# Keeping the split weights of the input and output projections in DRAM

## The chip, the cores and the metric

The kernel runs on one core of a Trainium2 chip. The metric is the time of one execution on the device, in microseconds (us). Three runs of the kernel before were timed; one more execution was recorded by the profiler, and all rows below are of that one.

## The reference

One layer of a hybrid decoder works on 2048 tokens of 1024 channels, in float32:

```
h    = rms_norm(x) * scale + shift
proj = h @ w_in                              # 1024 -> 3344 columns
o    = concat(gla(proj), rwkv7(proj))        # two recurrent mixers
x    = x + gate * (o @ w_out)                # 1024 -> 1024
x    = x + gate2 * conv_mlp(norm(x))         # gated MLP, width 2816
out  = rms_norm(x)
```

`scale`, `shift` and the gates come from one vector `c` through the modulation weights `ada_w`. The weights are the same for every token.

## The kernel before

**Split operands.** The projections want float32 accuracy from matmuls that take rounded operands (type `F32R`). So both sides are split into a high part, the rounded value, and a low part, the rest, and each product is three matmuls: high with high, low with high, high with low (`gemm3`, lines 258 to 265; the same three in `pair_gemm`, lines 431 to 433, and `values_tok`, lines 334 to 336).

**The class `Weights`** (lines 164 to 191) brings one tile of weights, 128 x 1024, in two halves of 128 x 512 (256 KB each). For each half a DMA on SyncE's queue (SP) fills a staging buffer `w_st` (line 174), ScalarE (ACT) casts it to the high part `w_hi` (line 179), and VectorE (DVE) or, every third time, GpSimd (POOL) subtracts to get the low part `w_lo` (line 182). In the first phase there are five staging buffers and three buffers each of `w_hi` and `w_lo` (line 158: `nst`, `nhl`). The modulation weights use the staging buffers too (`ada_dot`, line 200), without a split.

**Order of the work.** The tokens are four blocks of 512 (`NBLK`). First the modulation of block 0 is computed, with its Q, K and V projections straight from `w_first` (lines 533 to 560). Then `stage_b(b)` (lines 345 to 390) makes the other projections of a block: 18 tiles of `w_in` in block 0; 22 tiles of `w_in` and four tiles of `w_v` in blocks 1 to 3, so that every tile is loaded and split again in each block. The first two and the last two tiles of a block go in pairs (`pair_gemm`, lines 422 to 434), which ask for single halves (`cols=NB`). The results go to DRAM (`evacuate`).

The mixers work on 16 units of 128 tokens, `gla` (lines 610 to 726) and `rwkv_p`, `rwkv_i`, `rwkv_j`, `rwkv_s` (lines 751 to 1029). The projections of the next block are the filler between their steps: `fill()` (lines 395 to 408) advances `stage_b` by so many tiles per step. A unit's inverse goes out to DRAM and back twice, in other layouts (`inv_a`, lines 844 to 848; `inv_y`, lines 884 to 888), with DMAs on the same queue of SP. The modulation weights of the later stages are read five tiles per unit in the first units (`ada_rest`). When no block is left to project, the output projection `stage_d` (lines 436 to 471) of blocks 0 to 2 is the filler (`spare`, lines 1039 to 1046): eight tiles of `w_out` per block, split again for each.

The second phase, from line 1082 on, is the MLP, with other pools and buffers (line 1098: nine staging buffers and four each of `w_hi` and `w_lo`). The output projection of block 3 runs inside it (`d_begin`, line 1417), with `Weights` taking from these pools.

**What sets the order.** Each engine works through its instructions in a fixed order; the framework chooses it when the program is built, from priorities (`tc.cur_priority`, which `fill` sets back by `lag`) and its own estimate of when an instruction is ready. Waits between engines are semaphores. All DMAs here are issued by SP, in order, so one that waits holds up those behind it.

Of the kernel before, what the change touches and what calls it, by code (L numbers as in the profile page):

```python
# [9 lines left out]
F32 = mybir.dt.float32  # L10
F32R = mybir.dt.float32r
# [5 lines left out]
P = 128  # L17
D = 1024
KT = 8
NB = 512  # L20
# [9 lines left out]
TQ, TK, TV, TG, TZ, TR, TRK, TRV, TWA, TPG = 0, 2, 4, 8, 12, 13, 17, 21, 25, 26  # L30
# [65 lines left out]
def hybrid_kernel(ctx, tc, x, cst, vec, c_row, ada_t, w_in, w_v, w_first, w_z, gk_up, wa_up, g_up,  # L96
                  w_out, ffn_up, ffn_down, out, T=2048):
    nc = tc.nc
    NBLK = T // NB
# [55 lines left out]
        return ct[:, o - P:o - P + w]  # L155

    pools["w"] = ph1.enter_context(tc.tile_pool(name="wp1", bufs=2))
    pools["np"], pools["nst"], pools["nhl"], pools["nev"], pools["nx"] = 2, 5, 3, 3, 2
    pools["h"] = ph1.enter_context(tc.tile_pool(name="hp1", bufs=1))
    pools["hb"] = 9  # L160

    split_n = [0]

    class Weights:

        def __init__(self, src, split=True, cols=1024):
            n = pools["np"]
            step = 1024 // n
            self.step = step
            self.st, self.hi, self.lo = [], [], []  # L170
            for i in range((cols + step - 1) // step):
                w = min(step, cols - i * step)
                t = pools["w"].tile([P, step], F32, name="w_st", tag="wst", bufs=pools["nst"])
                nc.sync.dma_start(out=t[:, 0:w], in_=src[:, i * step:i * step + w])
                self.st.append(t)
                if split:
                    hi = pools["w"].tile([P, step], F32R, name="w_hi", tag="whi", bufs=pools["nhl"])
                    lo = pools["w"].tile([P, step], F32R, name="w_lo", tag="wlo", bufs=pools["nhl"])
                    A.copy(out=hi[:, 0:w], in_=t[:, 0:w])  # L179
                    split_n[0] += 1  # L180
                    eng = G if split_n[0] % 3 == 0 else V
                    eng.tensor_tensor(out=lo[:, 0:w], in0=t[:, 0:w], in1=hi[:, 0:w].bitcast(F32), op=ALU.subtract)  # L182
                    self.hi.append(hi)
                    self.lo.append(lo)

        def cut(self, which, a, n):
            i = a // self.step
# [68 lines left out]
    step = [0]  # L256
# [66 lines left out]
    def values_tok(b, h, i):  # L323

        bks = [gbank(), gbank()]
        for c in range(2):
            w = Weights(w_v[i, c])
            parts_ = [(k, t) for k in range(4) for t in range(4)] if c == 0 else [(k, t) for p_ in range(2) for k in range(4) for t in (2 * p_, 2 * p_ + 1)]
            for k, t in parts_:
                tc.cur_priority += step[0] // 4  # L330
                wh, wl = w.pair(k * 256, 256)
                hi, lo = (a_[:, t * P:(t + 1) * P] for a_ in h[4 * c + k])
                o_ = bks[t // 2][:, (t % 2) * 256:(t % 2) * 256 + 256]
                PE.matmul(out=o_, lhsT=hi, rhs=wh, start=c == 0 and k == 0 and t % 2 == 0, stop=False)
                PE.matmul(out=o_, lhsT=lo, rhs=wh, start=False, stop=False)
                PE.matmul(out=o_, lhsT=hi, rhs=wl, start=False, stop=c == 1 and k == 3 and t % 2 == 1)
            if c == 0:
                yield
        for p_ in range(2):
            ev = ap.tile([P, NB], F32, name="ev", tag="ev", bufs=pools["nev"])  # L340
            A.copy(out=ev, in_=bks[p_])
            nc.sync.dma_start(out=pd[b][TV][:, 2 * p_:2 * p_ + 2, i * 256:(i + 1) * 256], in_=ev.rearrange("p (t c) -> p t c", t=2))
        yield

    def stage_b(b):

        h = ahead.pop(b)[1]
        order = ([TZ] + list(range(8, TZ)) if b == 0 else list(range(8)) + [TZ] + list(range(8, TZ))) + [TWA, TPG] + [TR + i for i in range(12)]
        for i_, t in enumerate(order):
            if b + 1 < NBLK:  # L350
                if i_ == len(order) - 15:
                    ahead[b + 1] = stats_a(b + 1)
                if i_ == len(order) - 11:
                    stats_b(b + 1)
                if i_ == len(order) - 7:
                    stage_a(b + 1, range(0, EXTRA))
                if i_ == len(order) - 2:
                    stage_a(b + 1, range(EXTRA, KT))
            if t == TZ:

                ps = gbank()
                w = Weights(w_z, split=False, cols=KT * 32)
                for i in range(2):
                    for p_ in range(2):
                        for j in range(4):
                            k = 4 * i + j
                            PE.matmul(out=ps[32 * j:32 * j + 32], lhsT=w.cut(w.st, k * 32, 32), rhs=h[k][p_].bitcast(F32),
                                      start=i == 0 and p_ == 0, stop=i == 1 and p_ == 1)
                ev = ap.tile([P, NB], F32, name="ev", tag="ev", bufs=pools["nev"])
                A.activation(out=ev, in_=ps, func=AF.Identity, bias=vcol("zone"))  # L370
                nc.sync.dma_start(out=pd[b][TZ][:, 0, :], in_=ev)
                yield
                continue
            if TV <= t < TG:
                if (t - TV) % 2 == 0:
                    yield from values_tok(b, h, (t - TV) // 2)
                continue
            if b > 0 and i_ < 2:
                if i_ == 0:
                    bks = pair_gemm(w_in[0], w_in[1], h)  # L380
                ps = bks[i_]
            elif b + 1 < NBLK and i_ >= len(order) - 2:
                if i_ == len(order) - 2:
                    bks = pair_gemm(w_in[t - 1], w_in[t], h)
                ps = bks[i_ - len(order) + 2]
            else:
                ps = gbank()
                gemm3(ps, Weights(w_in[t if t < TZ else t - 1]), h)
            evacuate(b, t, ps)
            yield  # L390

# [27 lines left out]
            V.tensor_tensor(out=lo, in0=m, in1=hi.bitcast(F32), op=ALU.subtract)  # L419
        return h  # L420

    def pair_gemm(wa, wb, h):

        bks = [gbank(), gbank()]
        for c in range(2):
            ws = [Weights(w_[:, c * NB:(c + 1) * NB], cols=NB) for w_ in (wa, wb)]
            for k in range(4):
                hi, lo = h[4 * c + k]
                for ps, w in zip(bks, ws):
                    wh, wl = w.pair(k * P, P)  # L430
                    PE.matmul(out=ps, lhsT=wh, rhs=hi, start=c == 0 and k == 0, stop=False)
                    PE.matmul(out=ps, lhsT=wh, rhs=lo, start=False, stop=False)
                    PE.matmul(out=ps, lhsT=wl, rhs=hi, start=False, stop=c == 1 and k == 3)
        return bks

    def stage_d(b, h, acc=None, pair=False, before=None, after=None):
        if acc is None:
            acc = ap.tile([P, NB], F32, name="x_ss", tag="ns", bufs=1)
        bks = None
        for ft in range(KT):  # L440
            if pair and ft >= KT - 2:
                if bks is None:
                    if before is not None:
                        before()
                    bks = pair_gemm(w_out[ft], w_out[ft + 1], h)
                ps = bks[ft - KT + 2]
                if ft == KT - 1:
                    bks = None
            elif pair and ft < 2:
                if ft == 0:  # L450
                    bks = pair_gemm(w_out[0], w_out[1], h)
                ps = bks[ft]
                if ft == 1:
                    bks = None
            else:
                ps = gbank()
                gemm3(ps, Weights(w_out[ft]), h)
            if ft == 0 and after is not None:
                after()
            xr = ap.tile([P, NB], F32, name="xr", tag="xt", bufs=pools["nx"])  # L460
            nc.sync.dma_start(out=xr, in_=x[ft, :, b * NB:(b + 1) * NB])
            V.scalar_tensor_tensor(out=xr, in0=ps, scalar=mod[:, 16 + ft:17 + ft], in1=xr, op0=ALU.mult, op1=ALU.add)
            add_square(ap, acc, xr, ft == 0, G)
            nc.sync.dma_start(out=x2d[b][:, ft, :], in_=xr)
            if ft < KT - 1:
                yield
        fin = lambda: rstd_tok(rn2[:, b], sum_tok(acc))
        if pair:
            return fin
        yield  # L470
        fin()
# [31 lines left out]
    for i in range(4):  # L503
        hv, t_ = halves(i, "x0")
# [28 lines left out]
    for k in range(KT):  # L533
# [8 lines left out]
        hi, lo = hpair()  # L542
# [1009 lines left out]
```

## Time and profile before

| | us |
|---|---|
| median of 3 runs | 2959.83 |
| lowest and highest | 2950.89, 2960.01 |
| profiled execution | 2950.25 |
| its span, from the first to the last instruction | 2948.5 |

TensorE has two rows in the profile: PE is matmuls, PEld weight loads, which overlap them. A name with a small q (SPq) is an engine's queue of instructions. PEclk or "granted clock" is the share of full speed that TensorE had. In a group, "idle before" is the time that the engine stood idle just ahead of these instructions, followed by what ended it. The chain of waits goes back from the last instruction, at each step to what released it. L179 is line 179 of the kernel before. The execution runs in these stretches: opening and Q, K, V of block 0 until about 85 us; the other projections of block 0 until about 255; the mixers with the projections of blocks 1 to 3 until about 1090; the mixers with the output projection until about 1440; then the MLP, with the output projection of block 3 around 2090 to 2180.

### The profile page before, as it was taken

What the parts mean: (1) busy time and instruction counts of PE and PEld (TensorE: products, weight loads), DVE (VectorE), ACT (ScalarE), POOL (GpSimd) and SP (SyncE); (2) the same over time, 40 slices, a digit from 0 to 9 for tenths busy, and PEclk for the clock granted to TensorE, in tenths of its full rate; (3) what the DMA queues carried; (4) which work ended last, traced back from release to release, by engine and by line L of the source; (5) the groups of instructions that cost most, each with busy time, mean ns of one, the idle gap of its engine ahead of it and who ended that gap; (6) DMA issues with size and microseconds to landing.
All of it is one profiled execution on the core that took longest, in us unless ns stands there. A gap on an engine that the chain in (4) does not pass through costs nothing.

```text
span 2948.5 us, 54765 instructions
## 1 busy us (share of the span) xinstructions
PE 2764.5 (94%) x20296; PEld 2231.9 (76%) x20296; DVE 2198.3 (75%) x4229; ACT 1407.2 (48%) x2909; POOL 1189.5 (40%) x1212
## 2 busy tenths in 40 slices
PE   6998899999999999899869999999998999999998
PEld 5777777877777777777658788888776788888887
DVE  7368787777877677888587775866879786685867
ACT  4555445445554565555444353533545453353443
POOL 5224232323222233334455463544537454363541
PEclk9999999999989999989979999999998999999999
DMA  8556544544333334533415334243465534425243
GB/s 282 173 166 190 159 122 136 151 143 120 113 112 101 109 115 148 148 101 105 151 53 164 116 104 153 91 138 125 147 200 171 193 101 139 129 97 161 85 132 109
DMA packets 316875, 401.95 MB, mean 136 GB/s; under 512 B 75584, under 2 KB 148544, under 8 KB 316608
## 3 DMA queue, kind: packets, MB, share of 16 engines
q1 hardware_dynamic: 316608, 398.45, 43.2%
q8 instruction: 160, 2.62, 0.4%
q14 instruction: 107, 0.88, 0.1%
HBM read 293.49 MB, written 104.86 MB: 135 GB/s over the span
## 4 chain that ended last, share of the span: by engine, by line
PE 60%; DVE 15%; DMA 7%; issue 3%; ACT 2%; POOL 2%; SPq 0%; DVEq 0%; POOLq 0%; ACTq 0%
PE g_bank L1251 9%; PE g_bank L1249 9%; PE g_bank L1250 9%; PE g_bank L1306 5%; PE g_bank L1308 5%; PE g_bank L1307 5%; PE g_bank L263 3%; PE g_bank L265 3%; PE g_bank L264 3%; DMA w_st<-in_ada_t 1%; DVE w_lo L182 1%; PE gl_bank L679 1%; DMA x_k<-in_x 1%; DMA ub<-x 1%; DVE gl_d L652 1%
## 5 line engine op out<-in xcount | busy, mean ns | idle before, releaser
L1249 PE MATMUL g_bank<-h_hi,w_hi 128*128 128x512 f32 x1232 | 488.7, 397 | 29.0 <-ACT h_hi L1124 12.4
L1251 PE MATMUL g_bank<-h_hi,w_lo 128*128 128x512 f32 x1232 | 481.7, 396 | 16.8 <-POOL w_lo L1125 12.3
L1250 PE MATMUL g_bank<-h_lo,w_hi 128*128 128x512 f32 x1232 | 487.7, 396 | 7.7 <-DVE h_lo L1125 4.7
L1124 ACT CAST w_hi<-w_st 128x512 fp32r<-128x512 f32 (+1 forms) x396 | 239.1, 609 | 465.6 <-PE g_bank L1307 342.6
L1309 DVE SCALAR_TENSOR_TENSOR acc<-g_bank,mod,acc 128x512 f32<-128x512 f32 (+1 forms) x200 | 144.9, 729 | 249.5 <-PE g_bank L1308 234.5
L1125 POOL TENSOR_TENSOR w_lo<-w_st,w_hi 128x512 fp32r<-128x512 f32 x154 | 221.5, 1439 | 229.2 <-ACT w_hi L1124 225.5
L263 PE MATMUL g_bank<-h_hi,w_hi 128*128 128x512 f32 x736 | 299.3, 408 | 5.2 <-ACT carry L320 3.8
L265 PE MATMUL g_bank<-h_hi,w_lo 128*128 128x512 f32 x736 | 297.4, 405 | 3.5 <-DVE w_lo L182 3.5
L1249 PEld LDWEIGHTS g_bank<-h_hi,w_hi 128*128 128x128 f32 x1232 | 235.5, 191 | 84.3 <-ACT h_hi L1124 14.7
L264 PE MATMUL g_bank<-h_lo,w_hi 128*128 128x512 f32 x736 | 295.9, 402 | 0.0
L1251 PEld LDWEIGHTS g_bank<-h_hi,w_lo 128*128 128x128 f32 x1232 | 235.7, 191 | 71.6 <-POOL w_lo L1125 17.8
L1250 PEld LDWEIGHTS g_bank<-h_lo,w_hi 128*128 128x128 f32 x1232 | 235.8, 191 | 58.9 <-DVE h_lo L1125 5.7
L1306 PE MATMUL g_bank<-hh,w_hi 128*128 128x512 f32 x640 | 251.5, 395 | 4.7 <-DVE acc L1309 4.6
L1308 PE MATMUL g_bank<-hh,w_lo 128*128 128x512 f32 x640 | 251.5, 395 | 0.0
L1307 PE MATMUL g_bank<-hl,w_hi 128*128 128x512 f32 x640 | 251.4, 395 | 0.0
L179 ACT CAST w_hi<-w_st 128x512 fp32r<-128x512 f32 x272 | 167.6, 619 | 118.8 <-PE g_bank L264 59.9
L182 POOL TENSOR_TENSOR w_lo<-w_st,w_hi 128x512 fp32r<-128x512 f32 x90 | 128.3, 1425 | 228.6 <-ACT w_hi L179 191.5
L1125 DVE TENSOR_TENSOR w_lo<-w_st,w_hi 128x512 fp32r<-128x512 f32 (+1 forms) x242 | 201.1, 831 | 19.4 <-ACT w_hi L1124 19.4
L182 DVE TENSOR_TENSOR w_lo<-w_st,w_hi 128x512 fp32r<-128x512 f32 x182 | 142.2, 782 | 63.6 <-ACT w_hi L179 52.9
L263 PEld LDWEIGHTS g_bank<-h_hi,w_hi 128*128 128x128 f32 x736 | 141.1, 192 | 37.5 <-ACT carry L320 4.8
L265 PEld LDWEIGHTS g_bank<-h_hi,w_lo 128*128 128x128 f32 x736 | 141.1, 192 | 36.1 <-DVE w_lo L182 5.2
L264 PEld LDWEIGHTS g_bank<-h_lo,w_hi 128*128 128x128 f32 x736 | 141.6, 192 | 28.7 <-issue 0.5
(344 smaller groups left out, 6382.1 us busy)
## 6 DMA issues: line engine op xcount, KB each, us to landing
acc<-acc SPq DMA_DIRECT2D x352, 256.0 KB, 3.1
w_st<-in_ffn_up SPq DMA_DIRECT2D x176, 256.0 KB, 3.0
w_st<-in_w_in SPq DMA_DIRECT2D x168, 256.0 KB, 3.0
proj<-ev SPq DMA_DIRECT2D x100, 256.0 KB, 3.0
w_st<-in_ffn_down SPq DMA_DIRECT2D x80, 256.0 KB, 2.7
w_st<-in_ada_t SPq DMA_DIRECT2D x64, 256.0 KB, 3.4
w_st<-in_w_out SPq DMA_DIRECT2D x64, 256.0 KB, 3.1
x_k<-in_x SPq DMA_DIRECT2D x48, 256.0 KB, 3.7
```

Source lines behind the costliest of these rows:

```text
L182: eng.tensor_tensor(out=lo[:, 0:w], in0=t[:, 0:w], in1=hi[:, 0:w].bitcast(F32), op=ALU.subtract)
L263: PE.matmul(out=ps, lhsT=wh, rhs=hi, start=k == 0, stop=False)
L264: PE.matmul(out=ps, lhsT=wh, rhs=lo, start=False, stop=False)
L265: PE.matmul(out=ps, lhsT=wl, rhs=hi, start=False, stop=k == KT - 1)
L1124: A.copy(out=hi, in_=t)
L1125: eng.tensor_tensor(out=lo, in0=t, in1=hi.bitcast(F32), op=ALU.subtract)
L1249: PE.matmul(out=ps, lhsT=wh[:, c], rhs=hi, start=first and k == 0, stop=False, skip_group_check=True)
L1250: PE.matmul(out=ps, lhsT=wh[:, c], rhs=lo, start=False, stop=False, skip_group_check=True)
L1251: PE.matmul(out=ps, lhsT=wl[:, c], rhs=hi, start=False, stop=last and k == 3, skip_group_check=True)
L1306: PE.matmul(out=ps, lhsT=wh, rhs=hh, start=j == 0, stop=False)
L1307: PE.matmul(out=ps, lhsT=wh, rhs=hl, start=False, stop=False)
L1308: PE.matmul(out=ps, lhsT=wl, rhs=hh, start=False, stop=j == n - 1)
```

## The change

`Weights` gets a key for each tile. At the first use of a keyed half, the half is loaded and split as before, and its high and low parts are also stored in DRAM, in two tiles of 256 KB, by two more DMAs on SP. At a later use of the same key both parts are loaded straight into `w_hi` and `w_lo` by two DMAs, with no staging buffer, cast or subtraction. The last block stores nothing that no later block uses. The first projection of block 0 (`w_first`), the small weights `w_z` and the modulation weights have no key. The first phase has four staging buffers instead of five, and six buffers each of `w_hi` and `w_lo` instead of three.

```diff
--- before.py
+++ after.py
@@ -155,21 +155,32 @@
         return ct[:, o - P:o - P + w]
 
     pools["w"] = ph1.enter_context(tc.tile_pool(name="wp1", bufs=2))
-    pools["np"], pools["nst"], pools["nhl"], pools["nev"], pools["nx"] = 2, 5, 3, 3, 2
+    pools["np"], pools["nst"], pools["nhl"], pools["nev"], pools["nx"] = 2, 4, 6, 3, 2
     pools["h"] = ph1.enter_context(tc.tile_pool(name="hp1", bufs=1))
     pools["hb"] = 9
 
     split_n = [0]
 
+    kept = {}
+
     class Weights:
 
-        def __init__(self, src, split=True, cols=1024):
+        def __init__(self, src, split=True, cols=1024, key=None, at=0, keep=True):
             n = pools["np"]
             step = 1024 // n
             self.step = step
             self.st, self.hi, self.lo = [], [], []
             for i in range((cols + step - 1) // step):
                 w = min(step, cols - i * step)
+                if split and (key, at + i) in kept:
+                    pair = []
+                    for s_, from_ in zip(("hi", "lo"), kept[key, at + i]):
+                        t = pools["w"].tile([P, step], F32R, name="w_" + s_, tag="w" + s_, bufs=pools["nhl"])
+                        nc.sync.dma_start(out=t.bitcast(F32), in_=from_)
+                        pair.append(t)
+                    self.hi.append(pair[0])
+                    self.lo.append(pair[1])
+                    continue
                 t = pools["w"].tile([P, step], F32, name="w_st", tag="wst", bufs=pools["nst"])
                 nc.sync.dma_start(out=t[:, 0:w], in_=src[:, i * step:i * step + w])
                 self.st.append(t)
@@ -182,6 +193,13 @@
                     eng.tensor_tensor(out=lo[:, 0:w], in0=t[:, 0:w], in1=hi[:, 0:w].bitcast(F32), op=ALU.subtract)
                     self.hi.append(hi)
                     self.lo.append(lo)
+                    if key is not None and keep:
+                        to = []
+                        for s_, t in (("hi", hi), ("lo", lo)):
+                            d_ = dram.tile([P, step], F32, name=f"k{s_}_{len(kept)}")
+                            nc.sync.dma_start(out=d_, in_=t.bitcast(F32))
+                            to.append(d_)
+                        kept[key, at + i] = to
 
         def cut(self, which, a, n):
             i = a // self.step
@@ -324,7 +342,7 @@
 
         bks = [gbank(), gbank()]
         for c in range(2):
-            w = Weights(w_v[i, c])
+            w = Weights(w_v[i, c], key=("v", i, c), keep=b + 1 < NBLK)
             parts_ = [(k, t) for k in range(4) for t in range(4)] if c == 0 else [(k, t) for p_ in range(2) for k in range(4) for t in (2 * p_, 2 * p_ + 1)]
             for k, t in parts_:
                 tc.cur_priority += step[0] // 4
@@ -377,15 +395,16 @@
                 continue
             if b > 0 and i_ < 2:
                 if i_ == 0:
-                    bks = pair_gemm(w_in[0], w_in[1], h)
+                    bks = pair_gemm(w_in, 0, "in", h, b + 1 < NBLK)
                 ps = bks[i_]
             elif b + 1 < NBLK and i_ >= len(order) - 2:
                 if i_ == len(order) - 2:
-                    bks = pair_gemm(w_in[t - 1], w_in[t], h)
+                    bks = pair_gemm(w_in, t - 1, "in", h, b + 1 < NBLK)
                 ps = bks[i_ - len(order) + 2]
             else:
                 ps = gbank()
-                gemm3(ps, Weights(w_in[t if t < TZ else t - 1]), h)
+                t_ = t if t < TZ else t - 1
+                gemm3(ps, Weights(w_in[t_], key=("in", t_), keep=b + 1 < NBLK), h)
             evacuate(b, t, ps)
             yield
 
@@ -419,11 +438,11 @@
             V.tensor_tensor(out=lo, in0=m, in1=hi.bitcast(F32), op=ALU.subtract)
         return h
 
-    def pair_gemm(wa, wb, h):
+    def pair_gemm(wsrc, t0, name, h, keep):
 
         bks = [gbank(), gbank()]
         for c in range(2):
-            ws = [Weights(w_[:, c * NB:(c + 1) * NB], cols=NB) for w_ in (wa, wb)]
+            ws = [Weights(wsrc[t][:, c * NB:(c + 1) * NB], cols=NB, key=(name, t), at=c, keep=keep) for t in (t0, t0 + 1)]
             for k in range(4):
                 hi, lo = h[4 * c + k]
                 for ps, w in zip(bks, ws):
@@ -442,19 +461,19 @@
                 if bks is None:
                     if before is not None:
                         before()
-                    bks = pair_gemm(w_out[ft], w_out[ft + 1], h)
+                    bks = pair_gemm(w_out, ft, "out", h, True)
                 ps = bks[ft - KT + 2]
                 if ft == KT - 1:
                     bks = None
             elif pair and ft < 2:
                 if ft == 0:
-                    bks = pair_gemm(w_out[0], w_out[1], h)
+                    bks = pair_gemm(w_out, 0, "out", h, True)
                 ps = bks[ft]
                 if ft == 1:
                     bks = None
             else:
                 ps = gbank()
-                gemm3(ps, Weights(w_out[ft]), h)
+                gemm3(ps, Weights(w_out[ft], key=("out", ft)), h)
             if ft == 0 and after is not None:
                 after()
             xr = ap.tile([P, NB], F32, name="xr", tag="xt", bufs=pools["nx"])
```

## Rows read from the trace of the kernel before

**Rows 1.** The page: span, busy time of each engine, chain by engine.

```profile
span 2948.5 us, 54765 instructions
...
PE 2764.5 (94%) x20296; PEld 2231.9 (76%) x20296; DVE 2198.3 (75%) x4229; ACT 1407.2 (48%) x2909; POOL 1189.5 (40%) x1212
...
PE 60%; DVE 15%; DMA 7%; issue 3%; ACT 2%; POOL 2%; SPq 0%; DVEq 0%; POOLq 0%; ACTq 0%
```

**Rows 2.** Busy time by stage: PE, PEld, DVE, ACT, POOL, PEclk, DMA share, GB/s.

```profile
0.00:85.00 85.00, 59.41 (x252) 45.02 (x253) 59.53 (x88) 41.21 (x67) 38.53 (x37) 0.98 0.80 279
85.00:255.00 170.00, 159.12 (x1058) 128.42 (x1056) 102.95 (x248) 89.55 (x205) 49.98 (x67) 0.99 0.52 165
255.00:650.00 395.00, 366.26 (x4126) 296.26 (x4127) 306.48 (x832) 198.77 (x485) 119.83 (x142) 0.94 0.50 149
650.00:1090.00 440.00, 421.49 (x4714) 336.40 (x4713) 332.25 (x926) 236.23 (x588) 131.44 (x177) 0.95 0.37 110
1090.00:1440.00 350.00, 328.68 (x3816) 264.17 (x3816) 262.60 (x715) 184.55 (x462) 125.97 (x138) 0.93 0.43 130
1440.00:1540.00 100.00, 63.36 (x319) 47.65 (x318) 77.74 (x96) 46.36 (x80) 58.25 (x47) 0.76 0.28 87
```

**Rows 3.** The chain of waits from 255 to 1440 us, summed by line.

```profile
by line: PE g_bank L263 6.3%; PE g_bank L264 6.2%; PE g_bank L265 6.2%; issue 5.1%; DMA w_st<-in_ada_t 2.7%; DVE w_lo L182 2.2%; PE gl_bank L679 1.9%; DMA x_k<-in_x 1.9%; DVE gl_d L652 1.6%; PE rp_bank L113 1.4%; DMA inv_a<-rw_mab 1.4%; DVE
```

**Rows 4.** The page's costliest groups: the split of the weights.

```profile
L179 ACT CAST w_hi<-w_st 128x512 fp32r<-128x512 f32 x272 | 167.6, 619 | 118.8 <-PE g_bank L264 59.9
L182 POOL TENSOR_TENSOR w_lo<-w_st,w_hi 128x512 fp32r<-128x512 f32 x90 | 128.3, 1425 | 228.6 <-ACT w_hi L179 191.5
...
L182 DVE TENSOR_TENSOR w_lo<-w_st,w_hi 128x512 fp32r<-128x512 f32 x182 | 142.2, 782 | 63.6 <-ACT w_hi L179 52.9
```

**Rows 5.** Line 179 alone by stage: ACT busy (casts), PEclk, DMA share, GB/s.

```profile
85.00:255.00 170.00, 26.69 (x43) 0.99 0.52 165
255.00:650.00 395.00, 41.41 (x67) 0.94 0.50 149
650.00:1090.00 440.00, 46.50 (x75) 0.95 0.37 110
1090.00:1440.00 350.00, 31.90 (x52) 0.93 0.43 130
2090.00:2180.00 90.00, 9.61 (x16) 1.00 0.54 173
```

**Rows 6.** Line 263 (matmul): duration in ns, min/median/max.

```profile
L263 PE MATMUL g_bank<-h_hi,w_hi x736: 387/389/796, 82.4 to 2178.3; 128*128 128x512 f32 x184
```

**Rows 7.** Groups by line, 2090 to 2200 us: busy, mean ns, idle before, releaser.

```profile
L265 PE MATMUL g_bank<-h_hi,w_lo 128*128 128x512 f32 x64 | 25.3, 396 | 3.1 <-DVE w_lo L182 3.1
L263 PE MATMUL g_bank<-h_hi,w_hi 128*128 128x512 f32 x64 | 25.0, 391 | 1.1 <-ACT w_hi L179 1.1
```

**Rows 8.** DMA issues of the whole run: count, KB each, median us to landing.

```profile
w_st<-in_w_in SPq DMA_DIRECT2D x168, 256.0 KB, 3.0
...
w_st<-in_w_first SPq DMA_DIRECT2D x16, 256.0 KB, 6.1
...
rw_ln<-inv_a SPq DMA_DIRECT2D x32, 32.0 KB, 2.1
```

**Rows 9.** Line 174 on SP's queue: issue in ns, min/median/max, first and last start.

```profile
L174 SPq DMA_DIRECT2D w_st<-in_ada_t x64: 327/328/1298, 199.9 to 680.8; - x64
```

**Rows 10.** Waits of SP's queue, 255 to 1090 us: total us, times, longest.

```profile
SPq L174 <- DVE w_lo L182: 84.7, 44, 7.4
SPq L174 <- POOL w_lo L182: 45.6, 18, 6.4
```

**Rows 11.** Waits of ACT, 255 to 1090 us: total us, times, longest.

```profile
ACT w_hi L179 <- PE g_bank L264: 27.4, 21, 2.8
...
ACT w_hi L179 <- PE g_bank L335: 15.2, 13, 2.4
```

**Rows 12.** The chain in order of time: start us, us, what.

```profile
1441.86 5.63 DMA w_st<-in_ffn_up
```

## The prediction

> **What bounds the kernel now.** The page's first lines come first: of a span of 2948.5 us PE is busy 2764.5 us (94%), and the chain that ended last is 60% PE, 15% DVE, 7% DMA [rows 1]. A saving on ACT, DVE or POOL therefore counts only where PE is made to wait. The table of busy time by stage says where that is [rows 2]. I cut the span at 85, 255, 1440 and 1540 us: the opening, the projections of block 0 (from 85), the mixers with the projections of blocks 1 to 3 and the output projections beside them (255 to 1440), the change to the MLP. Before 255 us PE is short of full by 10.9 us only (159.12 of 170). From 255 to 1440 us it is busy 366.26 + 421.49 + 328.68 = 1116.4 of 1185 us: 68.6 us idle, with the granted clock at 0.94, 0.95 and 0.93 and DVE busy 306.48 + 332.25 + 262.60 = 901.3 us, 76%. This stage can gain from the change. The chain there is mixed: the three lines of the big matmuls have 19%, and of the work that the change removes the subtraction on DVE has 2.2%, 26 us of 1185 [rows 3]. So PE, DVE and waits take turns; no single engine bounds the stage.
>
> **What the change removes.** Splitting a half tile costs an ACT cast of 619 ns (272 of them) and a subtraction, 782 ns on DVE (182) or 1425 ns on POOL (90) [rows 4]. By the code, split work stays for the 16 halves of the first projection, 36 of block 0, 16 of block 1 (Q, K, V) and 16 of the output projection: 84. The other 188 become loads. The casts by stage are 43 from 85 to 255 us, 67 + 75 + 52 = 194 from 255 to 1440 us and 16 in the MLP's part [rows 5], so 272 - 210 = 62 lie before 255 us; 84 - 62 = 22 stay after it, and 172 of the 194 go. That is 172 x 0.619 = 106 us of ACT, 115 x 0.782 = 90 us of DVE and 57 x 1.425 = 81 us of POOL, all beside PE. What of it reaches the end? From below, nothing: PE would find the next late thing, the mixers' own DVE operations. From above, all idle time and what the low clock costs. DVE's busy share falls from 76% to 811/1185 = 68%; if waiting grows as share/(1 - share), which is my choice of a curve, it falls from 3.18 to 2.17, by 32%. 32% of 68.6 us is **22 us**; 89% of the chain's 26 us, 23 us, says the same by another way. I take 22.
>
> **The clock.** A 128x512 matmul takes 389 ns at the median and 796 ns at most [rows 6], which are the levels of 2.4 and 1.2 GHz. A mean grant of 0.94 over 1185 us is about 141 us at the lower level, so at most 70 us lost, PE's idle time included. Fewer gaps should raise the grant. 32% of 70 is 22 us; I take half, **11 us**, since a gap that only shrinks can still be followed by slow matmuls. Ends: 0 and 32 us.
>
> **The output projection inside the MLP.** Its last block has 16 halves. PE waited 3.1 us for the subtraction and 1.1 us for the cast there [rows 7]: **4 us** less. Each half now needs two loads into four buffers shared with the MLP's own weights, instead of one load into nine; a landing of 256 KB takes 3.0 us [rows 8], so two late ones would eat the gain (end: +6).
>
> **What it adds.** Each of the 188 halves loads twice, and 68 halves are stored in two parts: 188 + 136 = 324 transfers of 256 KB, 85 MB over the 402 moved now. In block 0 all is bunched: the 43 casts between 85 and 255 us bring 86 stores, 22.5 MB in 170 us, and 165 GB/s become about 298. The opening moves 279 GB/s at a DMA share of 0.80 [rows 2], and a weight load lands there in 6.1 us against 3.0 us elsewhere [rows 8]. Hidden by what? Loads run ahead by four staging and six split buffers, ten halves of twelve matmuls (4.7 us each), against three split buffers before. If that cover fails and the DMA stays at 279 GB/s, the 170 us become 182: +12. From below: the six buffers end the present waits of the cast for PE; but PE is full there, so 0. I take **+4**. Later the added transfers number 172 + 44 stores, 57 MB in 1185 us, 48 GB/s on about 129: no bound.
>
> SP's queue is the other cost. An issue takes 328 ns [rows 9], so 216 x 0.328 = 71 us more in the stage, on a queue where SP already stands still for 84.7 us behind DVE's subtraction and 45.6 us behind POOL's, before the loads of L174, from 255 to 1090 us alone [rows 10]. These waits go. In their place a kept load waits until PE has finished with the buffer six halves back, and what is queued behind it on SP waits too: the units' loads and the two trips through DRAM for the inverse. The nearest row for such a hold is ACT's wait for PE ahead of the cast: 27.4 + 15.2 us in 34 times, 1.25 us each, with three buffers [rows 11]. With six it should be rarer. Below zero is possible (holds vanish, ACT is freed); above see the rival. I take **+5**.
>
> The change to the MLP at 1440 us has PE busy 63.36 of 100 us [rows 2], and its chain starts with a 5.63 us weight load [rows 12]. The first pool of weights grows by 10 KB per partition, so the later pools wait for other tiles than before; I take 0, ends -6 and +6.
>
> **Sum.** -22 - 11 - 4 + 4 + 5 = -28 us. The profiled execution took 2950.25 us (span 2948.5), so 2922. The median of the three runs is 9.6 us above it (two near 2960, one at 2951); I add half: **2927 us**.
>
> **Rivals.** (1) **More comes free** than the 32%. Beside the splits the chain has 2.7% (32 us) on the staged loads of the modulation weights [rows 3]. They share the five staging buffers with the input projection, whose loads stand in the same queue. Kept halves leave that ring, so these 32 us can go as well, and the clock's 32 instead of 11: -22 - 32 - 32 - 4 + 4 + 5 = -81, 2869 + 5 = 2874. For it speaks that the waits named for L174 are those of this ring; against it that the last of the modulation's loads is issued at 680.8 us [rows 9] and that PE idles only 28.7 us up to 650. Chance 0.18.
>
> (2) **Hidden anyway.** PE is 94% busy, and the order of each engine is fixed when the program is built; PE could wait for the mixers' DVE operations as long as now. Then only the 4 us and the costs are left: 2950 + 5, 2955 to 2960. For it: 2.2% is all that the chain shows of the subtraction on DVE, and PE's own lines have 19%. Chance 0.14.
>
> (3) **Slower: SP's queue turns into the wait.** The place is L174 between 255 and 1440 us, the price h per hold. A unit passes SP at five places on its serial way (the load of its inputs, then out and back twice); the rows have 32 loads of rw_ln, two a unit, so 16 units and 80 places [rows 8]. If each meets one held load and half of that is covered by units prepared ahead, it costs 40h. It decides from 40h = 33 us (the gain without SP's 5 us), h = 0.83 us. At 1.5 us, somewhat over ACT's present 1.25: 2950 - 33 + 60 = 2977, and 2982 with the 5. For it: two parts per half wait for PE, in order, on a queue that already waits much. Against it: twice the buffers, and 130 us of other waits removed from the same queue. Chance 0.19.
> The Trainium skill (DMA: Bandwidth & Descriptors, Latency and other measured facts) gives an HBM access as 0.2 us on average and 2 us at high load: by it, an estimate, the 80 places at half cover cost up to 40 x 1.8 = 72 us, 2989 us. The opening's 6.1 against 3.0 us agrees in direction [rows 8]; no row shows the trips of the inverse under such load, so this adds to rival 3 and not to the sum.
>
> That the change does nothing is excluded: every later use has the key and the half of the first use, in pairs as well as in single tiles.
>
> **Numbers.** The forecast itself has 0.49, about 2905 to 2945. A difference of 0.3% (9 us) is about what the runs can tell from none; they span 9.1 us. Faster by more: 0.18 + 0.47 + a little of rival 2 = 0.66; within 0.3%: 0.15; slower: 0.19. The range goes from rival 1 (2875) up to nearly rival 3 at h = 1.5: 2875 to 2975.
>
> **What would show it.** Right: 84 casts on L179 and as many subtractions; DVE busy about 90 us less from 255 us on; PE idle in that stage near 47 us and the granted clock above 0.95; SP's waits behind the subtractions nearly gone; block 0 as long as now. Wrong: PE's idle time in the stage unchanged with other releasers (rival 2); SP's waits for PE's matmuls before the kept loads, and DVE waiting longer for rw_ln and rw_y (rival 3); block 0's projections ending 10 us later with landings near 6 us (the store's cover).

## The result

The changed kernel took 2935.04 us at the median of six runs, the kernel before 2949.32 us beside it. The ratio is 0.9941, with a 95% interval of 0.9921 to 0.996: 0.6% less time, some 17 us. The forecast was 2927 us, 0.8% below the 2950 us of the profiled execution; its sum had 28 us less.

**The profile after.** First the page of the changed kernel: span, busy time by engine, the chain by engine. They answer to [rows 1].

```profile
span 2925.2 us, 54728 instructions
...
PE 2751.4 (94%) x20296; PEld 2229.9 (76%) x20296; DVE 2085.8 (71%) x4103; ACT 1298.4 (44%) x2721; POOL 1088.3 (37%) x1150
...
PE 69%; DVE 13%; DMA 9%; ACT 3%; issue 3%; POOL 2%; SPq 0%; DVEq 0%; POOLq 0%; ACTq 0%
```

DVE, ACT and POOL each work 100 to 113 us less. PE's share of the span is what it was. The chain's shares, 69% for PE instead of 60%, cannot be set side by side as they stand: in the kernel before the chain can be followed back to 302 us only, where its first piece (start, length) is

```profile
301.96 4.54 DMA rw_k<-proj
```

while in the changed kernel it goes back to the start, through the opening and block 0. From 320 us to the first matmul of the MLP, with the pieces added up, PE has 47% of the chain before and 55% after, and DVE 28% and 18%.

Fixed cuts in time no longer fit, since every stage moves. I cut both traces at events instead: the first matmul of block 0's projections (L263, in the changed kernel L281), the first of the value projection of block 1 (L334, now L352) and the first of the MLP (L1249, now L1268). The first of these for the kernel before is in [rows 6]. The column after the durations is the first and last start, us. Before:

```profile
L334 PE MATMUL g_bank<-w_hi,h_hi x192: 274/283/467, 252.0 to 910.5; 128*128 128x256 f32 x192
L1249 PE MATMUL g_bank<-h_hi,w_hi x1232: 387/389/797, 1454.6 to 2889.7; 128*128 128x512 f32 x176
```

After:

```profile
L281 PE MATMUL g_bank<-h_hi,w_hi x736: 386/390/796, 80.6 to 2152.5; 128*128 128x512 f32 x184
L352 PE MATMUL g_bank<-w_hi,h_hi x192: 274/283/582, 240.6 to 891.2; 128*128 128x256 f32 x192
L1268 PE MATMUL g_bank<-h_hi,w_hi x1232: 387/389/797, 1423.3 to 2867.0; 128*128 128x512 f32 x176
```

Busy time between these cuts, kernel before (columns as in [rows 2]):

```profile
82.40:252.00 169.60, 161.25 (x1071) 130.30 (x1067) 99.95 (x245) 89.24 (x205) 47.49 (x66) 0.99 0.52 167
252.00:1454.60 1202.60, 1125.72 (x12795) 904.68 (x12794) 910.84 (x2485) 627.91 (x1551) 389.23 (x465) 0.94 0.44 131
1454.60:2948.50 1493.90, 1420.74 (x6196) 1154.06 (x6196) 1127.97 (x1413) 649.52 (x1090) 714.22 (x646) 0.97 0.41 130
```

and changed kernel:

```profile
80.60:240.60 160.00, 148.77 (x908) 121.72 (x905) 82.84 (x199) 77.13 (x179) 40.79 (x56) 0.96 0.93 321
240.60:1423.30 1182.70, 1126.91 (x12963) 911.99 (x12961) 824.09 (x2414) 539.94 (x1401) 307.08 (x417) 0.95 0.59 181
1423.30:2925.20 1501.90, 1419.42 (x6194) 1153.54 (x6192) 1117.97 (x1403) 640.36 (x1075) 701.22 (x642) 0.97 0.41 132
```

All that was won was won before the MLP: 31.3 us, of which the MLP's part gives 8.0 us back. The first stretch is 9.6 us shorter, but it holds 163 PE instructions fewer and the second 168 more: the mixers' work moved across the cut. So the first two belong together: 1372.2 us became 1342.7. PE's idle time in them fell from 85.2 to 67.0 us, and its busy time, for as many matmuls, from 1287.0 to 1275.7 us.

### The profile page after: what moved, and what is told of

It reads as the page before. It is cut to its first block, busy times and chain, and to the rows that moved or that the text cites. A ratio compares the mean times of both kernels' runs of the same rounds, so it can differ in the third digit from the quotient of the medians.

```text
span 2925.2 us, 54728 instructions
## 1 busy us (share of the span) xinstructions
PE 2751.4 (94%) x20296; PEld 2229.9 (76%) x20296; DVE 2085.8 (71%) x4103; ACT 1298.4 (44%) x2721; POOL 1088.3 (37%) x1150
## 4 chain that ended last, share of the span: by engine, by line
PE 69%; DVE 13%; DMA 9%; ACT 3%; issue 3%; POOL 2%; SPq 0%; DVEq 0%; POOLq 0%; ACTq 0%
PE g_bank L1270 9%; PE g_bank L1268 9%; PE g_bank L1269 9%; PE g_bank L1325 5%; PE g_bank L1327 5%; PE g_bank L1326 5%; PE g_bank L281 4%; PE g_bank L283 4%; PE g_bank L282 4%; PE gl_bank L698 1%; DMA rw_k<-proj 1%; DMA acc<-acc 1%; PE g_bank L450 1%; DMA w_st<-in_ada_t 1%; PE g_bank L452 1%
## 5 line engine op out<-in xcount | busy, mean ns | idle before, releaser
L1268 PE MATMUL g_bank<-h_hi,w_hi 128*128 128x512 f32 x1232 | 488.0, 396 | 26.6 <-ACT h_hi L1143 14.8
L1144 POOL TENSOR_TENSOR w_lo<-w_st,w_hi 128x512 fp32r<-128x512 f32 x154 | 219.3, 1425 | 241.7 <-ACT w_hi L1143 237.9
L281 PE MATMUL g_bank<-h_hi,w_hi 128*128 128x512 f32 x736 | 299.0, 406 | 8.0 <-DMA w_hi<-khi 3.8
L1268 PEld LDWEIGHTS g_bank<-h_hi,w_hi 128*128 128x128 f32 x1232 | 235.1, 191 | 81.6 <-ACT h_hi L1143 18.0
L1325 PE MATMUL g_bank<-hh,w_hi 128*128 128x512 f32 x640 | 251.9, 396 | 6.0 <-DVE acc L1328 6.0
L281 PEld LDWEIGHTS g_bank<-h_hi,w_hi 128*128 128x128 f32 x736 | 140.3, 191 | 41.6 <-issue 4.5
L1325 PEld LDWEIGHTS g_bank<-hh,w_hi 128*128 128x128 f32 x640 | 120.1, 188 | 37.3 <-DVE acc L1328 6.9
L1327 PEld LDWEIGHTS g_bank<-hh,w_lo 128*128 128x128 f32 x640 | 120.2, 188 | 29.4
L1326 PEld LDWEIGHTS g_bank<-hl,w_hi 128*128 128x128 f32 x640 | 120.2, 188 | 29.1
```

The costliest lines, as they stand in the source:

```text
L281: PE.matmul(out=ps, lhsT=wh, rhs=hi, start=k == 0, stop=False)
L1144: eng.tensor_tensor(out=lo, in0=t, in1=hi.bitcast(F32), op=ALU.subtract)
L1268: PE.matmul(out=ps, lhsT=wh[:, c], rhs=hi, start=first and k == 0, stop=False, skip_group_check=True)
L1325: PE.matmul(out=ps, lhsT=wh, rhs=hh, start=j == 0, stop=False)
L1326: PE.matmul(out=ps, lhsT=wh, rhs=hl, start=False, stop=False)
L1327: PE.matmul(out=ps, lhsT=wl, rhs=hh, start=False, stop=j == n - 1)
```

## The experiments

Four theories were to be told apart. **Theory 1**, the prediction's: time freed on DVE, ACT and POOL shortens PE's waits. **Theory 2**: the deeper buffers do it, since ACT no longer stands behind PE. **Theory 3**: SP's queue, held by loads that wait for PE, decides. **Theory 4**, formed after the first four kernels: any edit gives every engine a new order, and the order moves the time as much as the change does. Ratios are to the kernel before, run on the same chips; its median there was 2958 to 2961 us.

### The buffers alone

```diff
-    pools["np"], pools["nst"], pools["nhl"], pools["nev"], pools["nx"] = 2, 5, 3, 3, 2
+    pools["np"], pools["nst"], pools["nhl"], pools["nev"], pools["nx"] = 2, 4, 6, 3, 2
```

> The kernel before with four staging and six split buffers, and every half split at every use. Theory 1 (the gain is engine time freed on DVE, ACT and POOL from 255 us on): the split work stays, so 2943 to 2953 us beside a kernel before near 2949. Theory 2 (the gain is the deeper buffers, which free ACT from waiting for PE): near the changed kernel, 2930 to 2940 us.

Measured: 2989.05 us, ratio 1.0105 (1.0082 to 1.0128), about 31 us slower. Neither theory expected a loss. Theory 2 falls: the buffers by themselves give no gain in this order. The next run asks which of the two sizes it was, with five staging buffers and six split buffers:

```diff
-... = 2, 5, 3, 3, 2
+... = 2, 5, 6, 3, 2
```

> The kernel before with six split buffers and its five staging buffers; the run with four and six was 31 us slower than before. If the deeper split buffers cost that time (splits run further ahead of the mixers' work on ACT and DVE): again 25 to 35 us over before. If the lost staging buffer cost it (the ring shared with the modulation weights): within 5 us of before. If it is the chance of a new order: anything between.

Measured: 2986.12 us, 1.0087 (1.0066 to 1.0107). With the fifth staging buffer back the loss stays, so the lost buffer alone is not its cause. Busy time from the first value projection to the MLP, first for four and six, then for five and six buffers:

```profile
252.10:1490.30 1238.20, 1156.48 (x12869) 927.58 (x12867) 920.92 (x2497) 627.95 (x1557) 393.45 (x466) 0.93 0.42 125
```

```profile
258.10:1484.70 1226.60, 1145.42 (x12802) 923.88 (x12801) 917.42 (x2480) 622.17 (x1545) 386.55 (x466) 0.92 0.43 125
```

PE's busy time is 20 to 31 us above the 1125.72 of the kernel before for nearly the same number of instructions, and the granted clock is 0.93 and 0.92 against 0.94; idle time is 81.7 and 81.2 us against 76.9. More of the stage runs at the lower clock.

### The kept parts with the old buffers

```diff
-    pools["np"], pools["nst"], pools["nhl"], pools["nev"], pools["nx"] = 2, 4, 6, 3, 2
+    pools["np"], pools["nst"], pools["nhl"], pools["nev"], pools["nx"] = 2, 5, 3, 3, 2
```

(against the changed kernel)

> The changed kernel with the old buffers (five staging, three split). Theory 1: most of the gain stays unless the loads come late; with three buffers a kept load waits for PE three halves back and must land 3.5 us later, so 2935 to 2945 us. Theory 2: 2948 us or slower. Theory 3 (SP's queue behind PE decides): slower than before, above 2960 us.

Measured: 2963.89 us, 1.0021 (1.0004 to 1.0038). The split work is gone here as well, yet nothing is won. Its row for the same stage:

```profile
256.70:1456.70 1200.00, 1138.44 (x12814) 915.63 (x12812) 820.96 (x2391) 534.67 (x1384) 314.50 (x412) 0.94 0.58 179
```

DVE is as free as in the changed kernel (821 against 824 us), and PE idles 61.6 us; but PE is busy 13 us longer than before. So freed time on DVE is not by itself time won, and theory 1 as I put it is not enough. The number passes the 2960 us set for theory 3, but only beside a kernel before of 2958 us, which is no case for it. So neither half of the change gained alone, each run in one order. That they gain only together is not shown by it: in four orders the whole change lies between 0.9920 and 1.0039 (below), and 1.0021 is within that.

### The stores, with nobody reading them

```diff
-                if split and (key, at + i) in kept:
+                if False:
...
-                    if key is not None and keep:
+                    if key is not None and keep and (key, at + i) not in kept:
```

> The changed kernel with the stores, but later uses load and split as before, so the stores are pure cost on top of the deeper buffers. By my term for block 0: 4 us above the run with the buffers alone, all of it before 255 us, with the DMA share above 0.85 there. If the stores are hidden: equal to it within 3 us. If they crowd block 0: 10 us or more.

Measured: 2982.14 us, 1.0079 (1.006 to 1.0099), 0.3% below the buffers alone. The stores cost nothing that can be seen, although the DMA engines are near full in block 0's stretch:

```profile
85.00:255.00 170.00, 158.76 (x975) 131.05 (x974) 94.67 (x217) 84.44 (x191) 49.62 (x62) 0.95 0.92 317
```

This kernel and the changed one have the same buffers and stores and differ in what a later use does, split or load: 1.0079 against 0.9941, about 40 us. That is theory 1 at its strongest, among kernels with six buffers; but they differ in their order too, and the order alone moves the changed kernel by up to 1.2%, some 35 us (below).

### One load instead of two

```diff
-                    for s_, from_ in zip(("hi", "lo"), kept[key, at + i]):
+                    for s_, from_ in zip(("hi",), kept[key, at + i]):
...
-                    self.lo.append(pair[1])
+                    self.lo.append(pair[0])
```

> The changed kernel, but a later use loads the high part alone and takes it as the low part too (the low part is left out of the product, the matmuls stay). 188 loads of 256 KB less. If the second load (traffic, SP's issues) ate part of the gain: 8 to 20 us faster than the changed kernel, 2915 to 2927 us. If loads are hidden: 2931 to 2939 us.

Measured: 2921.86 us, 0.9881 (0.986 to 0.9902), 0.6% under the changed kernel's ratio, some 18 us. (The medians are 13 us apart, but the kernel before took 2949 us beside the changed kernel and 2958 us beside this one.) If that is the second load's price, it could be SP's issues or the bytes. The next run keeps the bytes and drops the issues:

```diff
...
+                    both = pools["w"].tile([P, 2, step], F32R, name="w_hl", tag="whl", bufs=pools["nhl"])
+                    nc.sync.dma_start(out=both.bitcast(F32), in_=kept[key, at + i])
...
+                        d_ = dram.tile([P, 2, step], F32, name=f"khl_{len(kept)}")
+                        nc.sync.dma_start(out=d_, in_=both.bitcast(F32))
...
```

> The changed kernel with both parts of a half side by side in one buffer, stored by one DMA and loaded by one of 512 KB in the first phase: same bytes, 68 stores and 172 loads less to issue on SP. If the 13 us between the changed kernel and the run with one load were SP's issues: 2920 to 2928 us. If they were bytes: 2931 to 2939 us. Slower, if a larger transfer lands later than PE wants it.

Measured: 2936.47 us, 0.9921 (0.99 to 0.9941). Against the changed kernel's 0.9941 (0.9921 to 0.996) that is no difference that can be told, so the issues are not shown to cost anything. Nor are the bytes: the 2936 us lie in the range set for the bytes, but that was set beside a kernel before of 2949 us, and 0.9921 of 2949 is 2926 us, in the range set for the issues. The gap of 0.6% stays within what a new order can do, as the next runs show.

### The same work in another order

The filler's priority is set back by 370; moving that number changes no instruction, only the order. Each of the two kernels was run with 350, 390 and 410.

```diff
-    filler, lag = [None], [370]
+    filler, lag = [None], [390]
```

> The kernel before with the same step of the filler's priority, 390 for 370. Little effect of the order: 2944 to 2958 us. Chance of the order as large as the change: 2930 to 2985 us.

> The changed kernel with the filler's priority set back by 390 instead of 370, which does the same work in another order. If the order alone moves the time little, 2930 to 2942 us. If the change's 16 us lie within what a new order does by chance, it lands anywhere from 2925 to 2965 us.

> The kernel before with the filler's priority set back by 350. At 390 a new order alone cost 0.6%. Theory 1 (the change saves engine time in any order): this and its partner with the change differ by 16 us or more, the partner faster. Theory 4 (order decides, the change saves little): this alone lands within 2945 to 2985 us, and the pair differs by under 8 us or the other way.

> The changed kernel with 350. Theory 1: 16 us or more below its partner. Theory 4: within 8 us of it, or above it.

> The kernel before with 410; as with 350: theory 1 wants it 16 us or more above its partner with the change, theory 4 within 8 us or below it.

> The changed kernel with 410. Theory 1: 16 us or more below its partner. Theory 4: within 8 us of it, or above it. Should either changed kernel lie under 2930 us it beats all so far.

The ratios to the kernel before, their quotient, and the first matmul of the MLP in the profiled executions:

```
set back by   unchanged (95%)          changed (95%)            quotient   MLP begins, us
350           1.0020 (1.0005-1.0035)   0.9920 (0.9900-0.9941)   0.990      1465.7 -> 1428.5
370           1                        0.9941 (0.9921-0.9960)   0.994      1454.6 -> 1423.3
390           1.0059 (1.0038-1.0079)   1.0039 (1.0023-1.0055)   0.998      1465.0 -> 1468.2
410           1.0004 (0.9988-1.0021)   0.9989 (0.9972-1.0006)   0.9985     1462.7 -> 1444.6
```

An order by itself moves the kernel before by up to 0.6% and the changed kernel by up to 1.2%, twice the change's own effect. The quotient is below 1 in all four orders, 0.49% on average (some 14 us), clearly so at 350 and 370; at 390 and 410 the intervals overlap. Theory 1 asked for 16 us or more in each pair: 32 us came at 350, 7 at 410 and 3 at 390. So theory 4 is right on the size of one measurement. On the direction the four orders agree with theory 1, but the quotients scatter by 0.4%, and four of them do not exclude a mean of no gain.

The traces show more than the times. Busy time from the first matmul of block 0's projections to the first of the MLP, each pair before and after, at 350, 370, 390 and 410 (columns as in [rows 2]):

```profile
83.00:1465.70 1382.70, 1291.25 (x13865) 1039.89 (x13861) 1000.20 (x2728) 714.01 (x1753) 436.35 (x531) 0.94 0.45 134
81.10:1428.50 1347.40, 1275.64 (x13864) 1035.64 (x13860) 917.56 (x2613) 620.33 (x1579) 347.35 (x472) 0.95 0.63 197
82.40:1454.60 1372.20, 1286.97 (x13864) 1034.98 (x13860) 1010.79 (x2729) 717.15 (x1754) 436.71 (x530) 0.95 0.45 135
80.60:1423.30 1342.70, 1275.69 (x13869) 1033.70 (x13865) 906.93 (x2612) 617.07 (x1579) 347.87 (x472) 0.95 0.63 197
82.20:1465.00 1382.80, 1305.39 (x13753) 1042.87 (x13749) 1018.68 (x2723) 713.28 (x1745) 437.52 (x529) 0.94 0.45 134
80.60:1468.20 1387.60, 1301.31 (x13769) 1049.31 (x13765) 917.55 (x2609) 618.70 (x1575) 354.07 (x475) 0.93 0.61 191
82.80:1462.70 1379.90, 1287.03 (x13769) 1035.37 (x13765) 1010.96 (x2725) 714.48 (x1748) 442.02 (x532) 0.95 0.45 134
80.80:1444.60 1363.80, 1290.62 (x13784) 1043.59 (x13780) 908.06 (x2608) 619.34 (x1578) 349.63 (x473) 0.94 0.62 195
```

The first number behind each stretch is its length, the next PE's busy time; their difference is PE's idle time:

```
set back by   PE idle, us    PE busy, us         DVE in the chain, 320 us to the MLP, us
350           91.5 -> 71.8   1291.3 -> 1275.6    245 -> 179
370           85.2 -> 67.0   1287.0 -> 1275.7    314 -> 202
390           77.4 -> 86.3   1305.4 -> 1301.3    298 -> 267
410           92.9 -> 73.2   1287.0 -> 1290.6    362 -> 210
```

In three of the four orders the change takes 18 to 20 us of idle time from PE, as theory 1 has it. At 390 it does not, though DVE is as free as in the others; the profiled execution of that order's unchanged kernel was the fastest of its eight (2967 us, the median is 2976), so this pair looks worse than its medians. PE's busy time is a second term, and it goes its own way, from 15.6 us less to 3.6 us more, with a granted clock that rises at 350 and falls at 390 and 410. At 410 this and a longer MLP eat most of what the idle time gave.

The chain agrees: from 320 us to the MLP, PE's share of it goes from 53 to 59%, 47 to 55%, 51 to 51% and 41 to 56% in the four orders. The share does not give the time by itself: with the old buffers it is 57% and nothing is won, with the packed parts 49%, and that kernel is fast.

## Why the prediction was right, step by step

**The count of the splits: right.** 84 casts and 56 + 28 subtractions remain, in place of the 272, 182 and 90 of [rows 4]. Groups by line of the changed kernel:

```profile
L190 ACT CAST w_hi<-w_st 128x512 fp32r<-128x512 f32 x84 | 50.9, 618 | 33.9 <-DMA w_st<-in_w_in 14.1 <-PE g_bank L282 8.8 <-DMA w_st<-in_w_first 2.9
...
L193 DVE TENSOR_TENSOR w_lo<-w_st,w_hi 128x512 fp32r<-128x512 f32 x56 | 43.0, 773 | 47.6 <-ACT w_hi L190 44.4 <-DMA khi<-w_hi 2.0 <-DMA klo<-w_lo 0.7
...
L193 POOL TENSOR_TENSOR w_lo<-w_st,w_hi 128x512 fp32r<-128x512 f32 x28 | 40.3, 1438 | 94.4 <-ACT w_hi L190 71.7 <-DMA khi<-w_hi 21.9 <-DVE gl_d L671 0.5
```

DVE is busy 87 us less between the value projection and the MLP (910.84 to 824.09), ACT 88 and POOL 82; I had 90, 106 and 81.

**The 22 us of PE's idle time: right in three orders of four. The 11 us of the clock: the size came in this order, the cause is not shown.** Over the first two stretches idle time fell by 18.2 us, block 0's 2.9 us more included, so by 21 us in the mixers' stage. Busy time fell by 11.3 us for as many matmuls. But the granted clock over both stretches together is 0.95 before and after, and in the other orders busy time moved by -15.6, -4.1 and +3.6 us: that this term came out at 11 has to do with the order, which is luck. The curve that I chose, share/(1 - share), is not confirmed either: at 390 DVE has the same free time, and PE's idle time rose from 77.4 to 86.3 us.

**Block 0, +4 us: the size was right for PE's idle time.** It rose from 8.4 to 11.2 us (by 2.0, 6.1 and 2.5 us at 350, 390 and 410). The granted clock of the stretch fell as well, from 0.99 to 0.96, which the term did not have; that is worth at most 0.03 x 160 = 4.8 us, an estimate from these rows. At 350 and 390 it is 0.97 with and without the change. Traffic was higher than my 298 GB/s (321, DMA share 0.93), and a weight load landed later than the 3.0 us of [rows 8]. DMA issues of the whole run of the changed kernel, with the median us to landing last:

```profile
w_hi<-khi SPq DMA_DIRECT2D x188, 256.0 KB, 3.5
w_lo<-klo SPq DMA_DIRECT2D x188, 256.0 KB, 3.8
...
khi<-w_hi SPq DMA_DIRECT2D x68, 256.0 KB, 3.8
...
w_st<-in_w_in SPq DMA_DIRECT2D x44, 256.0 KB, 4.7
```

In this stretch alone the loads of `w_in` land in 4.7 us too, against 3.0 before. The cover held: the loads run far enough ahead. One reading under it was wrong. The 389 ns of [rows 6] is the length of one matmul's record, and the records overlap: in block 0 of the kernel before, matmuls in a row start 0.23 us apart (start and length, us), so twelve take 2.8 us and not 4.7:

```profile
120.67 0.39 PE L263 MATMUL g_bank<-h_hi,w_hi 128*128 128x512 f32 x1
120.90 0.39 PE L264 MATMUL g_bank<-h_lo,w_hi 128*128 128x512 f32 x1
121.13 0.39 PE L265 MATMUL g_bank<-h_hi,w_lo 128*128 128x512 f32 x1
```

Block 0 uses a half every 4.7 us all the same (169.6 us for 36), because the mixers' matmuls stand in between: of the 1071 in the stretch 432 are of the 36 halves.

**SP's queue, +5 us, and rival 3: the hold came, its price did not.** Waits of SP's queue in the changed kernel, 240.6 to 1423.3 us:

```profile
SPq L179 <- PE g_bank L283: 130.0, 72, 12.9
...
SPq L179 <- PE g_bank L282: 29.1, 13, 8.4
...
SPq L179 <- PE g_bank L452: 19.5, 13, 4.8
```

These alone are 98 holds of 1.8 us, over the 0.83 us from which I had rival 3 win. What failed in the rival is its half of 80 places on the path. DVE's waits for the inverse's trips hardly changed; before, over the whole run:

```profile
DVE rw_pr L882 <- DMA rw_ln<-inv_a: 34.5, 12, 5.4
...
DVE rw_z L898 <- DMA rw_y<-inv_y: 24.5, 12, 4.1
```

and after:

```profile
DVE rw_pr L901 <- DMA rw_ln<-inv_a: 26.7, 11, 4.0
...
DVE rw_z L917 <- DMA rw_y<-inv_y: 26.5, 12, 4.3
```

By the code the units are prepared two ahead, and SP's holds took the place of others: from the first value projection to the MLP SP stood still behind the subtractions for 155 us before and 3 us after, behind PE's matmuls for 71 and 300 us, and for 888 and 777 us in all. No run prices the +5 by itself. The page of the Trainium skill on DMA (DMA: Bandwidth & Descriptors, Latency and other measured facts), by which HBM accesses slow down under load, agrees in direction with the landings of block 0, 4.7 us instead of 3.0; the 72 us that I had estimated from it did not come.

**The output projection inside the MLP, -4 us: wrong.** This step failed: the sum took away the waits for the split and put no wait for the kept load in their place. The waits for the split are gone, and PE waits 4.7 us, nearly all for the kept load, in place of the 4.2 us of [rows 7]. Groups by line of the changed kernel, 2060 to 2170 us:

```profile
L281 PE MATMUL g_bank<-h_hi,w_hi 128*128 128x512 f32 x64 | 25.2, 394 | 4.7 <-DMA w_hi<-khi 3.8 <-DVE xr L481 0.9
L283 PE MATMUL g_bank<-h_hi,w_lo 128*128 128x512 f32 x64 | 25.1, 393 | 0.0
```

**The rest of the MLP's part: not in the sum.** In the profiled executions of the four pairs the part from the MLP's first matmul to the end is 8.0, 10.3, 3.4 and 9.6 us longer with the change (for 370, 350, 390 and 410). Where, at 370, show cuts at the first matmul of the MLP's second projection (L1306, now L1325) and at the first and last of the output projection. Before:

```profile
1454.60:1561.20 106.60, 75.73 (x273) 57.59 (x274) 91.37 (x113) 51.86 (x88) 57.41 (x50) 0.79 0.17 54
1561.20:2124.60 563.40, 559.74 (x2437) 456.03 (x2435) 408.45 (x505) 240.44 (x403) 274.80 (x256) 1.00 0.42 130
2124.60:2179.10 54.50, 50.54 (x217) 40.41 (x218) 49.06 (x62) 27.02 (x46) 21.20 (x14) 1.00 0.67 212
2179.10:2948.50 769.40, 734.74 (x3273) 600.03 (x3271) 579.10 (x735) 330.19 (x556) 360.81 (x327) 0.97 0.42 134
```

After:

```profile
1423.30:1533.30 110.00, 73.83 (x270) 55.63 (x269) 94.20 (x114) 52.62 (x89) 57.57 (x51) 0.79 0.19 57
1533.30:2098.80 565.50, 560.01 (x2438) 456.43 (x2436) 410.98 (x508) 240.40 (x403) 277.17 (x256) 1.00 0.41 131
2098.80:2153.40 54.60, 51.76 (x225) 41.84 (x226) 33.85 (x49) 18.46 (x29) 10.69 (x9) 1.00 0.85 287
2153.40:2925.20 771.80, 733.82 (x3265) 599.64 (x3263) 578.93 (x735) 328.88 (x556) 355.79 (x327) 0.97 0.41 133
```

The output projection took 54.5 us before and 54.6 after: the 4 us did not come, and the 8.0 us are elsewhere. Of these, 3.4 us are at the change to the MLP, a term that the prediction took at 0 with ends of 6; 2.1 us lie between it and the output projection, and 2.4 us behind. At 390 and 410 the output projection is 3.0 and 5.0 us longer, nearer to the other end, +6, that the prediction gave the term. What lengthens the rest is open. Kept loads are not needed for it: the kernel with unused stores has none, and its MLP's part is 1500.5 us (2980.0 less 1479.5), 6.6 us above the 1493.9 of the kernel before. And the unchanged kernel's own part is 1491.8 to 1500.6 us in the four orders.

**The sum.** -28 was forecast. The profiled executions differ by -23.2 us (2927.03 and 2950.25): -29.5 before the MLP, -1.8 in the opening, +8.0 after. The sum had -24 before the MLP (-22 - 11 + 4 + 5) and -4 in it, so two errors cancel in part. The medians, which average over more, differ by 14 to 17 us. Part of the good fit is the order, which is luck: over the four the mean is 14 us.

Of the other rivals, the second (hidden anyway) is close to the times of the orders 390 and 410, but at 410 not by its mechanism, since PE's idle time fell there by 19.7 us. The first (81 us) is far from all four.

Two things stay open. Why deeper split buffers slow the kernel that still splits: the extra time is PE's at a lower granted clock, but which engine brings that about was not taken apart. And whether the 0.6% by which the run with one load lies lower are the load or the order. No version with the whole product was clearly under the changed kernel; the packed parts (0.9921) and the setting of 350 (0.9920) lie at the edge of its interval.

## What to carry to other kernels

Where a program is ordered as a whole when it is built, run the kernel before and after in a few orders that mean nothing before believing a difference of half a per cent; here four were too few to settle its size. Read the idle time and the busy time of the busiest engine separately: the one fell as forecast in three orders, the other moved by as much with the order. Before two chains are compared by their shares, look how far back each goes. Price a freed engine by the stage in which PE waits for it, and a held queue by who is late behind it, not by the length of the hold.

## What was not expected

Six split buffers in place of three cost 0.8 to 1.05% in three kernels that still split at every use (1.0105, 1.0087, 1.0079, each in one order), more than the kernel before moved in any of four orders. The DMA engines carried 321 GB/s at a share of 0.93 over 160 us beside PE, which idled only 11.2 us of them.
